# A two-layer decoder trunk on one core: the constants move from 13 loads on GpSimd's queue to 5 on the sync queue, and layer 0's x^T is rounded as it is loaded

## The chip, the cores and the metric

The kernel runs on one core of a Trainium2 chip. The metric is the time of one execution in device microseconds (us). Several executions are timed and the median is given; one more execution is taken with the hardware profiler, and its profile is the one shown here. The engines are named as in the profile: PE (TensorE, matrix products), PEld (its weight loads), DVE (VectorE), ACT (ScalarE), POOL (GpSimd) and SP (SyncE, which only starts transfers). "SPq" and "POOLq" are the queues on which SP and POOL start DMAs.

## What is computed

Two layers of a decoder trunk, on 256 positions of width 2048, in float32. Each layer normalises x, projects it by one large matrix, mixes in four ways side by side, and adds the result, projected back, to x:

```
for l in range(DEPTH):                       # 2
    h = rms_norm(x, norm_g[l])
    p = split_columns(h @ w_in[l])           # 2048 -> 18 column groups, 7700 wide
    fox  = softmax attention with a forget gate,  times silu(fox_g)
    diff = rms_norm(softmax map 1 - lam * softmax map 2) v, times silu(diff_g)
    moba = causal softmax attention with rotary,  times silu(moba_g)
    gla  = rms_norm(chunked gated linear attention), times silu(gla_g)
    x = x + concat(fox, diff, moba, gla) @ w_out[l]      # 2048 -> 2048
return rms_norm(x, final_norm_g)
```

The small parameters beside the two matrices are `fox_fb` (a bias of fox's forget gate), `diff_lam` (from which `lam` is made), `diff_norm_g`, `gla_norm_g`, and `gla_wa2` and `gla_ba` (GLA's gate).

## The kernel before, in words

**Products in float32 by three passes.** PE multiplies rounded numbers (float32r). Each weight tile `raw` is rounded on ACT into `hi` (`hi_of`), and DVE takes the rest, `lo = raw - hi` (`lo_of`). The transposed activations are split in the same way, into the two halves of `hTp`. A product is then hi by hi, lo by hi and hi by lo, 12 matmuls for a step of two k-tiles of 128 and both halves of the rows.

**The plan.** `_steps` (L176) lists the steps in the order in which PE does them. A step is two k-tiles of one block of columns. Layer 0 begins with the three narrow blocks (348, 512 and 348 columns, containing GLA's gate, q, k and fox's forget gate), taken k-tile by k-tile because x^T arrives piece by piece: 24 steps. Then come the blocks named in `MIDDLE` (L40), one after the other, 8 steps each, and the four blocks of `w_out`, whose later k-tiles wait for the later groups in the order gla, fox, diff, moba (`OUT_ORDER`). The first three steps are treated in halves (`HALVED`).

**Pairs and forms.** Some blocks, two in layer 0's and three in layer 1's `NAMES` (L41), are computed two at a time from seven products of sums ("forms", p1 to p7) in place of eight. Their names stand in `MIDDLE` but make no steps of their own. Their steps, 28 for each pair, are put among the others at the places in `FORMS_AT` (L43). The sums of activations that the forms need are made by `sum_forms` (L1687) from the scaled x^T (`env["t", l, c]`) into `mTh` and `mTl`. A second set of weights, `ys`, which lies in the tile `xs`, is loaded by `load_y` (L1549) up to `EARLY` steps ahead of the front of the loads, and changed by DVE and by accumulating DMAs as the forms go on.

**Who orders the other engines.** The program is written out by a planner that keeps a model of time (`Times`, `emit`, `choose`). Between groups of six matmuls, `fill` (L516) gives ACT and DVE work: the rounding of the next steps' weights goes first if it is urgent (`URGENT_HI`, `URGENT_LO`, `split_for`, with `LEAD` for the three-stage splits of p7), and otherwise the heads of the tasks in the order of their ranks (gla, fox, diff, moba). A task's operation is let through once the planner believes its operands ready; for a load that is a modelled landing time (`CONSTANT` is 4.0). The engines then execute their instructions in the order written. `ahead` is 3: a step's weights are rounded at most three steps before PE needs them (`PART_BUFS` is 4).

**The queues.** Weights are loaded by SP (`load`, `load_pair`), six `raw` tiles in a ring, each load waiting for the rounding of what lay in its tile. SP also carries `x^T` (`load_x`), `ys`, and the writes to memory with which tiles are turned (`turned`); POOL's queue carries the reads back, the accumulating loads, and the constants.

**The constants.** The task `constants` (L689) begins once all of layer 0's x^T has been split in the program, at step 16: tables (`ct`: the identity, triangles, rotary tables), fox's bias `fb`, GLA's gate matrix `w3` in float32 (cleared, then six loads), which ACT and DVE round into `wa`. After the first RMS is known come masks, `diff_lam`, `dng`, `neg_b` and `gng`. All 13 loads are on POOL's queue.

**Layer 0's x^T.** It arrives in four chunks `xts[c]` of four k-tiles. For the first four k-tiles, `split_xt` (L1622) rounds with the scale (`norm_g`) in the instruction: `xt_hi` on ACT, `xt_lo` on DVE. For the others, `whole_xt` (L1604) first scales on ACT into a tile `env["t", 0, c]`, which is then rounded whole, two k-tiles at a time. `first_rms` (L1638), which PE's loop moves on once a step, scales the first chunk in the same way, squares each `xts[c]` in place and adds the squares up.

Almost every instruction is recorded at L482, the line in `emit` where operations are written out; the names of the tiles tell them apart. Tiles named `four` are slots of a general pool of 13.

Of the kernel before, what the change touches and what calls it, by code (L numbers as in the profile page):

```python
# [13 lines left out]
F32 = mybir.dt.float32  # L14
# [12 lines left out]
H = 4  # L27
# [9 lines left out]
WARM = (512,) * 7 + (256,)  # L37
HALVED = 3
X_AT = (5, 8, 11, 13)
MIDDLE = (('gla_v', 'diff_q', 'fox_k', 'diff_v', 'fox_q', 'fox_g', 'diff_g', 'diff_k', 'moba_k', 'moba_v', 'moba_q', 'fox_v', 'moba_g'), ('gla_v', 'diff_k', 'fox_k', 'fox_q', 'fox_v', 'moba_q', 'fox_g', 'diff_q', 'diff_g', 'moba_v', 'moba_k', 'moba_g', 'diff_v'))  # L40
NAMES = ((('diff_q', 'diff_k'), ('moba_v', 'diff_v')), (('diff_q', 'diff_k'), ('moba_v', 'diff_v'), ('moba_g', 'diff_g')))  # L41
PAIR = tuple(tuple(3 + MIDDLE[l].index(z) for names in NAMES[l] for z in names) for l in range(2))
FORMS_AT = ((29, 33, 37, 37, 38, 39, 39, 40, 41, 42, 43, 46, 47, 48, 49, 49, 50, 52, 54, 55, 56, 56, 57, 59, 60, 61, 62, 64, 66, 67, 69, 71, 72, 73, 73, 76, 77, 77, 79, 80, 81, 82, 83, 84, 86, 88, 90, 91, 92, 92, 92, 93, 94, 96, 96, 98), (27, 29, 29, 29, 30, 30, 30, 31, 32, 32, 32, 32, 33, 33, 35, 35, 36, 37, 37, 38, 39, 39, 39, 41, 42, 43, 43, 44, 45, 45, 46, 46, 47, 49, 50, 50, 51, 51, 51, 52, 53, 53, 54, 54, 55, 55, 56, 57, 58, 58, 59, 59, 60, 60, 61, 61, 62, 65, 65, 65, 66, 66, 66, 67, 68, 69, 70, 71, 72, 72, 72, 73, 74, 74, 75, 75, 76, 77, 78, 79, 80, 80, 81, 83))  # L43
FORM_ORDER = ("p1", "p5", "p3", "p6", "p7", "p2", "p4")

ADDED_BY_V = ("p1", "p2")
# [13 lines left out]
URGENT_LO = 2.5  # L60
STALL = 0.1
DELAY = 0.5
LEAD = 3.0
OVERLAP = 0.085
SAFE = 1.5
HANDOVER = 0.2
SOON = 0.5
WAITED = 0.3
EARLY = 8
LOADED = 6.0  # L70
WRITE = 7.0
READ = 5.0
# [170 lines left out]
def bcast_rows(ap1d, offset, n):  # L243
    return bass.AP(tensor=ap1d.tensor, offset=ap1d.offset + offset, ap=[[0, P], [1, n]])
# [142 lines left out]
def hybrid_trunk(  # L387
# [3 lines left out]
    xt: bass.AP,  # L391
    norm_gt: bass.AP,
    weights: bass.AP,
    fox_fb: bass.AP,
    diff_lam: bass.AP,
    diff_norm_gt: bass.AP,
    gla_wa2: bass.AP,
    gla_ba: bass.AP,
    gla_norm_gt: bass.AP,
    final_norm_g: bass.AP,  # L400
    const: bass.AP,
    const_b: bass.AP,
# [180 lines left out]
    def matmul(out, lhsT, rhs, start, stop, tiles=1, main=False, **kw):  # L583
        n = int(np.prod(rhs.shape[1:]))
        us = (n * 4 if lhsT.dtype == F32 else n + 32) / 2400.0 / tiles
        give(Op("t", partial(t_.matmul, out, lhsT, rhs, start=start, stop=stop, **kw), [rhs] if main else [lhsT, rhs],
                [] if main else [out], us))
        if main:
            times.end(out, times.now, "t")
# [54 lines left out]
        return z  # L644


    ct = cp.tile([P, CONST["f"].shape[1]], F32, name="ct")
    ngt = cp.tile([P, DEPTH, KT], F32, name="ngt")
    xs = big.tile([P, 2, D], F32, name="xs")

# [8 lines left out]
    fb = cp.tile([P, DEPTH, H], F32, name="fb")  # L659
    dng = cp.tile([P, DEPTH], F32, name="dng")  # L660
    gng = cp.tile([P, DEPTH], F32, name="gng")
# [27 lines left out]
    def constants():  # L689

        yield from until(("h", 0, 3))
        g_.move(ct, const, 4.5)
        g_.move(fb.rearrange("p l h -> p (l h)"), bcast_rows(fox_fb, 0, DEPTH * H), CONSTANT)
        given_out("loaded")
        w3 = s2.get([P, DEPTH, 256])
        g_.memset(w3, 0.0)
        for i in range(0, 96, 32):
            g_.move(w3[i:i + 16], gla_wa2.rearrange("l r e -> r l e"), CONSTANT)
            g_.move(w3[i + 16:i + 17].rearrange("p l e -> p (l e)"), gla_ba.rearrange("(o l) e -> o (l e)", o=1), CONSTANT)
        yield  # L700
        hi_of(wa, w3)
        yield
        lo_of(wa[64:96], w3[64:96], wa[64:96])
        s2.put(w3)
        given_out("constants")
        yield from until(("r", 0))
        c, n = CAT["masks"]
        mb = s4.get([P, n], BF16)
        g_.move(mb, const_b[:, c:c + n], CONSTANT)
        yield  # L710
        v_.tensor_copy(masks.rearrange("p l t -> p (l t)"), mb)
        s4.put(mb)
# [12 lines left out]
        s2.put(lp, lamt)  # L725
        yield
        a_.activation(ls2, ls2, AF.Exp)
        yield
        for l in range(DEPTH):
            li = 0.8 - 0.6 * math.exp(-0.3 * l)  # L730
            v_.scalar_tensor_tensor(lam[:, l:l + 1], ls2[:, l, 0:1], li, ls2[:, l, 1:2], op0=OP.add, op1=OP.subtract)
            v_.tensor_scalar(dng[:, l:l + 1], dng[:, l:l + 1], 1.0 - li, None, op0=OP.mult)
        given_out("lam")

    hTp = big.tile([P, KT, 2, SEQ], F32R, name="hTp")
# [12 lines left out]
    def hi_of(hi, src, scale=1.0):  # L748
        a_.activation(hi, src, AF.Copy, scale=scale)

    def lo_of(lo, src, hi):
        v_.tensor_sub(lo, src, hi.bitcast(F32))
# [884 lines left out]

    def first_rms():  # L1638

        def fold(t):  # L1640
            for n in (2, 1):
                v_.tensor_add(t[:, 0:n], t[:, 0:n], t[:, n:2 * n])

        for c in range(4):
            yield from until(("h", 0, c))
            if WHOLE and c == 0:
                whole_xt(range(4))
            a_.activation(xts[c], xts[c], AF.Square)
            if c in (1, 2):
                v_.tensor_add(xts[0], xts[0], xts[c])  # L1650
                s4.put(xts[c])
            if c > 1:
                fold(xts[0 if c == 2 else 3])
        v_.tensor_add(xts[0][:, 0], xts[0][:, 0], xts[3][:, 0])
        yield
        yield
        yield
        ps = side.get([P, 1024])
        for m in range(2):
            matmul(ps[:, m:m + 1], xts[0][:, 0, m * P:(m + 1) * P], one, True, True)  # L1660
        t = before_pow(ps[:, 0:2], 2, 1.0 / D)
        side.put(ps)
        s4.put(xts[0], xts[3])
        r = sm.tile([P, 2], F32, name="rstd", bufs=2)
        power(r, t, 2)
        know_rows(0, r)
# [20 lines left out]
    def sum_forms(l):  # L1687
# [3 lines left out]
            yield from until(("h", l, c))  # L1691
        yield from until(("r", l))
        yield
        z = yield from s4.take([P, 8, P])
        whole = [env["t", l, c] for c in range(4)] if l or WHOLE else None

        def sums(op, a, b):
            for i in range(2):
# [373 lines left out]
    while tasks:  # L2072
# [3 lines left out]
    final_rows(1, b["ps1"][:, :256])  # L2076


_INS = ["x", "xt", "norm_gt", "weights", "fox_fb", "diff_lam", "diff_norm_gt", "gla_wa2", "gla_ba", "gla_norm_gt",
        "final_norm_g", "const", "const_b"]  # L2080


# [23 lines left out]
```

## Time and profile before

| | us |
|---|---|
| median of 3 timed executions | 891.17 |
| lowest, highest | 890.27, 892.38 |
| the profiled execution | 888.25 |
| its span, first to last instruction | 886.5 |
| busy in it: PE, DVE, ACT, POOL | 871.6, 734.9, 585.3, 65.0 |

How to read the lines below: a row of the timeline or of a single engine gives the start in us from the span's start, the time in us, engine, line and operation, `out<-in`, the shapes, the count of merged instructions, and in brackets how long the engine had been idle and what ended that. A row of a stretch `A:B` gives its length, then the busy time of PE, PEld, DVE, ACT and POOL with the count of instructions, the granted clock of PE (1.00 is full), the mean busy share of the 16 DMA engines, and GB/s. A row of a queue gives packets, MB and the share of the engines' time. A row of waits gives the total in us, how often, and the longest. A row of the DMA issues gives the size of one and the us from issue to landing.

### The profile page before, as it was taken

The page shows a single profiled execution, that of the slowest core. Times are in us where ns is not written, and L with a number is a line of the kernel's source. Part 1 is how long each engine was busy: PE and PEld are TensorE (multiplying, and loading weights), DVE is VectorE, ACT ScalarE, POOL GpSimd, SP SyncE. Part 2 cuts the span into 40 slices and gives each one's busy share as a digit, 9 for nine tenths or more (in the row PEclk, how much of TensorE's full clock was granted, in tenths as well). Part 3 has the DMA queues.
Part 4 walks back from the last instruction along what each step waited for, and adds up shares of the span by engine and source line. Part 5 has one row for each costly group of instructions (what it writes and reads, how often), then busy time and mean ns, then how long its engine had stood idle before and what let it go on. Part 6 is the DMA issues. An engine that isn't in the chain of part 4 may idle for free.

```text
span 886.5 us, 12487 instructions
## 1 busy us (share of the span) xinstructions
PE 871.6 (98%) x4292; PEld 739.1 (83%) x4292; DVE 734.9 (83%) x974; ACT 585.3 (66%) x919; POOL 65.0 (7%) x96
## 2 busy tenths in 40 slices
PE   8999999999999999999999999999999999999896
PEld 5998888888887988888899888888888788888786
DVE  4879979899787997757668699999999998986483
ACT  6877955478586468735756994676667776767361
POOL 3010010001010001000000010001100100100100
PEclk9999999999999999999999999999999999999999
DMA  8878795668997675987879786689898998779822
GB/s 280 304 247 270 233 309 182 205 231 298 377 286 235 201 285 198 313 317 221 279 256 356 240 229 250 209 306 266 247 328 290 278 302 295 247 257 353 281 96 95
DMA packets 84663, 231.63 MB, mean 261 GB/s; under 512 B 9736, under 2 KB 29976, under 8 KB 84472
## 3 DMA queue, kind: packets, MB, share of 16 engines
q1 hardware_dynamic: 75064, 198.29, 65.1%
q0 software_dynamic: 9104, 31.75, 13.5%
q10 hardware_dynamic: 432, 0.80, 0.2%
q8 instruction: 33, 0.54, 0.2%
q14 instruction: 30, 0.25, 0.1%
HBM read 208.25 MB, written 22.55 MB: 260 GB/s over the span
## 4 chain that ended last, share of the span: by engine, by line
PE 93%; DVE 3%; issue 1%; DMA 1%; ACT 0%; SPq 0%; POOLq 0%; POOL 0%; DVEq 0%; ACTq 0%
PE mm L482 79%; PE side L482 14%; DVE lo L482 2%; DMA raw<-in_weights 1%; DVE four L482 1%; DVE tq L482 0%; DVE xs L482 0%; SPq L1596 0%; ACT four L482 0%; DVE eight L482 0%; ACT hi L482 0%; SPq L1543 0%; DVE mTl L482 0%; ACT mTh L482 0%; POOLq L2102 0%
## 5 line engine op out<-in xcount | busy, mean ns | idle before, releaser
L482 ACT ACTIVATE hi<-raw 128x1024 fp32r<-128x1024 f32 (+2 forms) x319 | 316.6, 1009 | 181.2 <-PE mm L482 92.5
L482 DVE TENSOR_TENSOR lo<-raw,hi 128x1024 fp32r<-128x1024 f32 (+2 forms) x319 | 363.0, 1154 | 64.6 <-ACT hi L482 59.1
L482 PE MATMUL mm<-hi,hTp 128*128 128x512 f32 (+1 forms) x1520 | 374.1, 380 | 3.0 <-ACT hi L482 2.6
L482 PEld LDWEIGHTS mm<-hi,hTp 128*128 128x128 f32 x1520 | 277.8, 188 | 55.8 <-ACT hi L482 4.6
L482 PE MATMUL mm<-lo,hTp 128*128 128x512 f32 (+1 forms) x760 | 206.1, 378 | 0.0
L482 PEld LDWEIGHTS mm<-lo,hTp 128*128 128x128 f32 x760 | 139.9, 188 | 25.3 <-DVE lo L482 0.3
L482 PE MATMUL mm<-hi,mTh 128*128 128x512 f32 (+1 forms) x352 | 99.8, 383 | 3.3 <-ACT mTh L482 2.5
L482 PE MATMUL mm<-hi,mTl 128*128 128x512 f32 (+1 forms) x352 | 99.0, 381 | 0.1
L482 PE MATMUL mm<-lo,mTh 128*128 128x512 f32 (+1 forms) x352 | 98.9, 381 | 0.0
L482 ACT ACTIVATE hi<-xs 128x1024 fp32r<-128x1024 f32 x60 | 63.2, 1060 | 20.8 <-PE mm L482 18.3
L482 PEld LDWEIGHTS mm<-hi,mTh 128*128 128x128 f32 x352 | 63.3, 188 | 15.4 <-ACT mTh L482 2.7
L482 PEld LDWEIGHTS mm<-lo,mTh 128*128 128x128 f32 x352 | 64.0, 188 | 13.6 <-DVE lo L482 1.1
L482 PEld LDWEIGHTS mm<-hi,mTl 128*128 128x128 f32 x352 | 64.2, 188 | 13.1 <-DVE mTl L482 0.5
L482 DVE TENSOR_TENSOR lo<-xs,hi 128x1024 fp32r<-128x1024 f32 x60 | 72.0, 1212 | 0.8 <-ACT hi L482 0.7
L482 POOL DMA_DIRECT2D four<-far x40 | 22.1, 553 | 488.6 <-DMA far<-four 174.4
L482 DVE TENSOR_TENSOR xs<-xs,raw 128x1024 f32<-128x1024 f32 x40 | 48.6, 1215 | 0.0
L482 PE MATMUL side<-four,four 128*128 128x128 f32 (+3 forms) x320 | 42.3, 298 | 0.0
L482 PEld LDWEIGHTS side<-four,four 128*128 128x128 f32 (+1 forms) x320 | 38.2, 190 | 4.6 <-issue 1.4
L482 DVE STREAM_TRANSPOSE four<-four 128x1024 f32<-128x1024 f32 (+1 forms) x34 | 38.7, 1140 | 3.7 <-ACT four L482 3.5
L482 ACT ACTIVATE four<-mm,rstd 128x512 f32<-128x512 f32 (+2 forms) x46 | 29.2, 663 | 14.6 <-PE mm L482 14.2
L482 ACT ACTIVATE four<-side 128x128 f32<-128x128 f32 (+3 forms) x66 | 16.0, 266 | 23.8 <-PE side L482 23.2
L482 ACT ACTIVATE four<-side,nb 128x128 f32<-128x128 f32 (+1 forms) x64 | 26.2, 417 | 4.2 <-DVE nb L482 4.2
(152 smaller groups left out, 715.6 us busy)
## 6 DMA issues: line engine op xcount, KB each, us to landing
raw<-in_weights SPq DMA_DIRECT2D x271, 512.0 KB, 5.0
four<-far POOLq DMA_DIRECT2D x34, 512.0 KB, 6.5
far<-four SPq DMA_DIRECT2D x128, 128.0 KB, 3.7
raw<-in_weights SPq DMA_DIRECT2D x46, 348.0 KB, 4.8
xs<-in_weights SPq DMA_DIRECT2D x20, 512.0 KB, 5.5
xs<-in_weights POOLq DMA_DIRECT2D x20, 512.0 KB, 8.7
xs<-in_x SPq DMA_DIRECT2D x4, 512.0 KB, 7.9
kept<-xs SPq DMA_DIRECT2D x1, 2048.0 KB, 8.4
```

The lines of the kernel that those rows point to most:

```text
L482: op.do()
```

## The change

Five things are changed together.

1. **Constants.** `fox_fb` (spread over the partitions), `diff_norm_g` and `gla_norm_g` are appended to the table on the host, so that `ct` is 12 columns wider and one load brings all of them. GLA's gate matrix with its bias is laid out on the host, zeros included, and loaded by one transfer. The loads are `ct`, `w3`, the masks, `diff_lam` and `neg_b`: five, all on SP's queue (`q_`) at the same places in the program.
2. **Layer 0's x^T.** All k-tiles are rounded by `xt_hi` and `xt_lo` straight from `xts`. `first_rms` squares into a tile of its own. A new task `scale_xt` scales each chunk in place after its Square, four instructions a chunk, and `sum_forms` waits for these.
3. **Order of the blocks.** `MIDDLE` is new for both layers.
4. **Places of the forms.** `FORMS_AT` is new: in layer 0 the first places move from 29 to 32 and others by up to three; in layer 1 two places move by one.
5. **Planner.** `LEAD` is 3.5 instead of 3.0, `EARLY` 3 instead of 8.

```diff
-MIDDLE = (('gla_v', 'diff_q', 'fox_k', 'diff_v', 'fox_q', 'fox_g', 'diff_g', 'diff_k', 'moba_k', 'moba_v', 'moba_q', 'fox_v', 'moba_g'), ('gla_v', 'diff_k', 'fox_k', 'fox_q', 'fox_v', 'moba_q', 'fox_g', 'diff_q', 'diff_g', 'moba_v', 'moba_k', 'moba_g', 'diff_v'))
+MIDDLE = (('gla_v', 'fox_k', 'diff_q', 'fox_q', 'diff_v', 'fox_g', 'diff_g', 'moba_v', 'moba_k', 'diff_k', 'fox_v', 'moba_q', 'moba_g'), ('gla_v', 'fox_k', 'diff_k', 'fox_q', 'fox_v', 'moba_q', 'fox_g', 'moba_v', 'diff_q', 'moba_k', 'diff_g', 'moba_g', 'diff_v'))
...
-LEAD = 3.0
+LEAD = 3.5
...
-EARLY = 8
+EARLY = 3
...
     def constants():
 
         yield from until(("h", 0, 3))
-        g_.move(ct, const, 4.5)
-        g_.move(fb.rearrange("p l h -> p (l h)"), bcast_rows(fox_fb, 0, DEPTH * H), CONSTANT)
+        q_.move(ct, const, CONSTANT)
         given_out("loaded")
         w3 = s2.get([P, DEPTH, 256])
-        g_.memset(w3, 0.0)
-        for i in range(0, 96, 32):
-            g_.move(w3[i:i + 16], gla_wa2.rearrange("l r e -> r l e"), CONSTANT)
-            g_.move(w3[i + 16:i + 17].rearrange("p l e -> p (l e)"), gla_ba.rearrange("(o l) e -> o (l e)", o=1), CONSTANT)
+        q_.move(w3.rearrange("p l e -> p (l e)"), gla_w, CONSTANT)
...
-        g_.move(mb, const_b[:, c:c + n], CONSTANT)
+        q_.move(mb, const_b[:, c:c + n], CONSTANT)
...
-        g_.move(lamt.rearrange("p l a d -> p (l a d)"), bcast_rows(diff_lam, 0, DEPTH * 256), CONSTANT)
-        g_.move(dng, diff_norm_gt, CONSTANT)
+        q_.move(lamt.rearrange("p l a d -> p (l a d)"), bcast_rows(diff_lam, 0, DEPTH * 256), CONSTANT)
         c, n = CAT["neg"]
-        g_.move(neg_b, const_b[:, c:c + n], CONSTANT)
-        g_.move(gng, gla_norm_gt, CONSTANT)
+        q_.move(neg_b, const_b[:, c:c + n], CONSTANT)
...
-    def whole_xt(kts):
-
-        for kt in kts:
-            if kt % 4 == 0:
-                env["t", 0, kt // 4] = s4.get([P, 4, SEQ])
-            a_.activation(env["t", 0, kt // 4][:, kt % 4], xts[kt // 4][:, kt % 4], AF.Copy, scale=ngt[:, 0, kt:kt + 1])
+    def scale_xt():
+
+        for c in range(4):
+            yield from until(("squares", c))
+            for k in range(4):
+                kt = c * 4 + k
+                a_.activation(xts[c][:, k], xts[c][:, k], AF.Copy, scale=ngt[:, 0, kt:kt + 1])
+                if k % 2:
+                    yield
+            env["t", 0, c] = xts[c]
+            given_out(("t", c))
...
     def split_xt(kts):
 
-        if WHOLE and kts[0] >= 4:
-            whole_xt(kts)
-            hi, lo = (z[:, kts[0]:kts[-1] + 1] for z in hT)
-            src = env["t", 0, kts[0] // 4][:, kts[0] % 4:kts[-1] % 4 + 1]
-            hi_of(hi, src)
-            lo_of(lo, src, hi)
-        else:
-            for kt in kts:
-                xt_hi(kt)
-            for kt in kts:
-                xt_lo(kt)
+        for kt in kts:
+            xt_hi(kt)
+        for kt in kts:
+            xt_lo(kt)
...
+        sq = {}
         for c in range(4):
             yield from until(("h", 0, c))
-            if WHOLE and c == 0:
-                whole_xt(range(4))
-            a_.activation(xts[c], xts[c], AF.Square)
+            sq[c] = (yield from s4.take([P, 4, SEQ])) if WHOLE else xts[c]
+            a_.activation(sq[c], xts[c], AF.Square)
+            if WHOLE:
+                given_out(("squares", c))
...
     begin(constants(), 0, 3)
+    if WHOLE:
+        begin(scale_xt(), 0, 3)
     begin(sum_forms(0), 0, 3)
```

More of the change, by code (lines that the diff above doesn't have):

```diff
@@ L39 @@
 X_AT = (5, 8, 11, 13)
-MIDDLE = (('gla_v', 'diff_q', 'fox_k', 'diff_v', 'fox_q', 'fox_g', 'diff_g', 'diff_k', 'moba_k', 'moba_v', 'moba_q', 'fox_v', 'moba_g'), ('gla_v', 'diff_k', 'fox_k', 'fox_q', 'fox_v', 'moba_q', 'fox_g', 'diff_q', 'diff_g', 'moba_v', 'moba_k', 'moba_g', 'diff_v'))
+MIDDLE = (('gla_v', 'fox_k', 'diff_q', 'fox_q', 'diff_v', 'fox_g', 'diff_g', 'moba_v', 'moba_k', 'diff_k', 'fox_v', 'moba_q', 'moba_g'), ('gla_v', 'fox_k', 'diff_k', 'fox_q', 'fox_v', 'moba_q', 'fox_g', 'moba_v', 'diff_q', 'moba_k', 'diff_g', 'moba_g', 'diff_v'))
 NAMES = ((('diff_q', 'diff_k'), ('moba_v', 'diff_v')), (('diff_q', 'diff_k'), ('moba_v', 'diff_v'), ('moba_g', 'diff_g')))
 PAIR = tuple(tuple(3 + MIDDLE[l].index(z) for names in NAMES[l] for z in names) for l in range(2))
-FORMS_AT = ((29, 33, 37, 37, 38, 39, 39, 40, 41, 42, 43, 46, 47, 48, 49, 49, 50, 52, 54, 55, 56, 56, 57, 59, 60, 61, 62, 64, 66, 67, 69, 71, 72, 73, 73, 76, 77, 77, 79, 80, 81, 82, 83, 84, 86, 88, 90, 91, 92, 92, 92, 93, 94, 96, 96, 98), (27, 29, 29, 29, 30, 30, 30, 31, 32, 32, 32, 32, 33, 33, 35, 35, 36, 37, 37, 38, 39, 39, 39, 41, 42, 43, 43, 44, 45, 45, 46, 46, 47, 49, 50, 50, 51, 51, 51, 52, 53, 53, 54, 54, 55, 55, 56, 57, 58, 58, 59, 59, 60, 60, 61, 61, 62, 65, 65, 65, 66, 66, 66, 67, 68, 69, 70, 71, 72, 72, 72, 73, 74, 74, 75, 75, 76, 77, 78, 79, 80, 80, 81, 83))
+FORMS_AT = ((32, 33, 35, 38, 39, 40, 41, 42, 43, 44, 45, 46, 47, 48, 49, 50, 52, 53, 54, 55, 56, 57, 58, 59, 60, 61, 62, 64, 67, 68, 69, 71, 72, 73, 73, 76, 77, 77, 79, 80, 81, 82, 83, 84, 86, 88, 90, 92, 93, 93, 93, 93, 95, 96, 97, 99), (27, 29, 29, 29, 30, 30, 30, 31, 32, 32, 32, 32, 33, 33, 35, 35, 36, 37, 37, 38, 39, 39, 39, 41, 42, 43, 44, 44, 45, 45, 46, 46, 47, 49, 50, 50, 51, 51, 51, 52, 53, 53, 54, 54, 55, 55, 56, 57, 58, 58, 59, 59, 60, 60, 61, 61, 62, 65, 65, 65, 66, 66, 66, 67, 68, 69, 70, 71, 72, 72, 72, 73, 74, 74, 75, 75, 76, 78, 78, 79, 80, 80, 81, 83))
 FORM_ORDER = ("p1", "p5", "p3", "p6", "p7", "p2", "p4")
@@ L393, in hybrid_trunk @@
     weights: bass.AP,
-    fox_fb: bass.AP,
     diff_lam: bass.AP,
[L396 to L399, printed above, removed]
+    gla_w: bass.AP,
     final_norm_g: bass.AP,
@@ L644, in put_in_order @@
         return z
-    ct = cp.tile([P, CONST["f"].shape[1]], F32, name="ct")
+    ct = cp.tile([P, CONST["f"].shape[1] + 12], F32, name="ct")
+    own = ct[:, CONST["f"].shape[1]:]
     ngt = cp.tile([P, DEPTH, KT], F32, name="ngt")
@@ L658, in hybrid_trunk @@
     masks = cp.tile([P, NL, 64], U8, name="masks")
-    fb = cp.tile([P, DEPTH, H], F32, name="fb")
+    fb = own[:, :8].rearrange("p (l h) -> p l h", h=H)
     dng = cp.tile([P, DEPTH], F32, name="dng")
-    gng = cp.tile([P, DEPTH], F32, name="gng")
+    gng = own[:, 10:12]
     wa = cp.tile([P, DEPTH, 256], F32R, name="wa")
@@ L731, in constants @@
             v_.scalar_tensor_tensor(lam[:, l:l + 1], ls2[:, l, 0:1], li, ls2[:, l, 1:2], op0=OP.add, op1=OP.subtract)
-            v_.tensor_scalar(dng[:, l:l + 1], dng[:, l:l + 1], 1.0 - li, None, op0=OP.mult)
+            v_.tensor_scalar(dng[:, l:l + 1], own[:, 8 + l:9 + l], 1.0 - li, None, op0=OP.mult)
         given_out("lam")
@@ L1642, in fold @@
                 v_.tensor_add(t[:, 0:n], t[:, 0:n], t[:, n:2 * n])
+        sq = {}
         for c in range(4):
             yield from until(("h", 0, c))
-            if WHOLE and c == 0:
-                whole_xt(range(4))
-            a_.activation(xts[c], xts[c], AF.Square)
+            sq[c] = (yield from s4.take([P, 4, SEQ])) if WHOLE else xts[c]
+            a_.activation(sq[c], xts[c], AF.Square)
+            if WHOLE:
+                given_out(("squares", c))
             if c in (1, 2):
-                v_.tensor_add(xts[0], xts[0], xts[c])
-                s4.put(xts[c])
+                v_.tensor_add(sq[0], sq[0], sq[c])
+                s4.put(sq[c])
             if c > 1:
-                fold(xts[0 if c == 2 else 3])
-        v_.tensor_add(xts[0][:, 0], xts[0][:, 0], xts[3][:, 0])
+                fold(sq[0 if c == 2 else 3])
+        v_.tensor_add(sq[0][:, 0], sq[0][:, 0], sq[3][:, 0])
         yield
@@ L1659, in first_rms @@
         for m in range(2):
-            matmul(ps[:, m:m + 1], xts[0][:, 0, m * P:(m + 1) * P], one, True, True)
+            matmul(ps[:, m:m + 1], sq[0][:, 0, m * P:(m + 1) * P], one, True, True)
         t = before_pow(ps[:, 0:2], 2, 1.0 / D)
         side.put(ps)
-        s4.put(xts[0], xts[3])
+        s4.put(sq[0], sq[3])
         r = sm.tile([P, 2], F32, name="rstd", bufs=2)
@@ L1693, in sum_forms @@
         yield
+        whole = None
+        if l or WHOLE:
+            for c in range(4 if not l else 0):
+                yield from until(("t", c))
+            whole = [env["t", l, c] for c in range(4)]
         z = yield from s4.take([P, 8, P])
-        whole = [env["t", l, c] for c in range(4)] if l or WHOLE else None
         def sums(op, a, b):
@@ L2076, in hybrid_trunk @@
     final_rows(1, b["ps1"][:, :256])
-_INS = ["x", "xt", "norm_gt", "weights", "fox_fb", "diff_lam", "diff_norm_gt", "gla_wa2", "gla_ba", "gla_norm_gt",
-        "final_norm_g", "const", "const_b"]
+_INS = ["x", "xt", "norm_gt", "weights", "diff_lam", "gla_w", "final_norm_g", "const", "const_b"]
 def kernel(**inputs):
@@ L2089 @@
     given["norm_gt"] = np.ascontiguousarray(g.reshape(DEPTH, KT, P).transpose(2, 0, 1))
-    for name in ("diff_norm_g", "gla_norm_g"):
-        given[name + "t"] = np.ascontiguousarray(given.pop(name).T)
+    gla_w = np.zeros((P, DEPTH, 256), np.float32)
+    for i in range(0, 96, 32):
+        gla_w[i:i + 16] = given["gla_wa2"].transpose(1, 0, 2)
+        gla_w[i + 16] = given["gla_ba"]
+    given["gla_w"] = gla_w.reshape(P, -1)
     given["xt"] = np.ascontiguousarray(given["x"][0].T.reshape(KT, P, SEQ).transpose(1, 0, 2))
     given["weights"] = in_steps(given.pop("w_in"), given.pop("w_out"))
-    given["const"], given["const_b"] = CONST["f"], CONST["b"]
+    own = [np.broadcast_to(given["fox_fb"].reshape(1, -1), (P, DEPTH * H)), given["diff_norm_g"].T, given["gla_norm_g"].T]
+    given["const"], given["const_b"] = np.concatenate([CONST["f"], *own], 1), CONST["b"]
     nc = bacc.Bacc("TRN2", target_bir_lowering=False, num_devices=1, dynamic_dma_scratch_size=4096)
```

## The prediction

> **What bounds the kernel now.** I read the page's busy times first, then the busy time by 20 us stretches, then the chain and the timelines of single engines where PE was idle.
>
> ```profile
> PE 871.6 (98%) x4292; PEld 739.1 (83%) x4292; DVE 734.9 (83%) x974; ACT 585.3 (66%) x919; POOL 65.0 (7%) x96
> ```
> ```profile
> 0.00:20.00 20.00, 16.00 (x64) 10.67 (x65) 8.35 (x17) 12.28 (x22) 7.40 (x18) 1.00 0.85 283
> ...
> sum 460.00, PE 456.00 PEld 385.41 DVE 369.18 ACT 308.20 POOL 35.28; mean PE 19.83 PEld 16.76 DVE 16.05 ACT 13.40 POOL 1.53
> ```
> ```profile
> 860.00:886.50 26.50, 19.18 (x160) 18.98 (x159) 10.75 (x24) 4.95 (x9) 2.04 (x3) 0.92 0.21 80
> sum 426.50, PE 415.58 PEld 353.71 DVE 365.70 ACT 277.06 POOL 29.72; mean PE 19.79 PEld 16.84 DVE 17.41 ACT 13.19 POOL 1.42
> ```
>
> PE sets the time. In the first 460 us it is idle for 460.00 - 456.00 = 4.0 us, and all of that lies in the first 20 us (20.00 - 16.00). In the other 426.5 us it is idle for 10.9 us, 7.3 of them in the last 26.5, where the output is written. So work that comes off ACT, DVE or a queue in the middle of the kernel is worth nothing; a stall that goes in the first 20 us is worth its length, because everything behind it is a full PE. The start is the place to look:
>
> ```profile
> 14.46 1.52 PE L482 MATMUL mm<-hi,hTp 128*128 128x348 f32 x8 [0.21 <-ACT hi L482]
> 15.82 0.79 PE L482 MATMUL mm<-lo,hTp 128*128 128x348 f32 x4
> 18.10 2.12 PE L482 MATMUL mm<-hi,hTp 128*128 128x512 f32 x8 [1.49 <-ACT hi L482]
> ```
> ```profile
> 11.54 1.09 ACT L482 ACTIVATE hi<-raw 128x348 fp32r<-128x348 f32 x2 [1.65 <-DMA raw<-in_weights]
> 12.54 0.89 ACT L482 ACTIVATE hTp<-four,ngt 128x256 fp32r<-128x256 f32 x2
> 13.63 0.79 ACT L482 ACTIVATE hi<-raw 128x696 fp32r<-128x696 f32 x1 [0.19 <-DMA raw<-in_weights]
> 14.32 1.69 ACT L482 ACTIVATE four<-four,ngt 128x256 f32<-128x256 f32 x4
> 16.04 1.06 ACT L482 ACTIVATE four<-four 128x1024 f32<-128x1024 f32 x1
> 17.01 1.72 ACT L482 ACTIVATE hi<-raw 128x1024 fp32r<-128x1024 f32 x2
> 18.63 0.89 ACT L482 ACTIVATE four<-four,ngt 128x256 f32<-128x256 f32 x2
> 19.55 0.63 ACT L482 ACTIVATE hTp<-four 128x512 fp32r<-128x512 f32 x1
> ```
>
> These are steps 3 and 4 of the plan. Up to 13.6 us each rounding on ACT waits for its weights to land (1.65 us, 0.19 us): the DMA sets the pace. Then ACT does four scalings of x^T and a Square (14.32 to 17.10) ahead of the rounding that step 4 needs, and PE, done with step 3 at 15.82 + 0.79 = 16.61, stands for 1.49 us.
>
> **The change part by part.**
>
> *The four scalings leave the start.* They took ACT from 14.32 to 16.04, 1.72 us. The Square stays, now into a tile of its own. The rounding for step 4 then starts at 17.01 - 1.72 = 15.29 instead of 17.01. PE took it up 18.10 - 17.01 = 1.09 us after it began, so it could begin at 16.38; it is busy with step 3 until 16.61. What is late next is PE itself, so the gain is the whole gap and no more: **1.49 us**.
>
> *Eight loads of the constants leave the start.* Before, they stand in GpSimd's queue, which has nothing to wait for, and so run at once, although the program puts them behind step 16.
>
> ```profile
> ct<-in_const POOLq DMA_DIRECT2D x1, 289.0 KB, 6.3
> ```
> ```profile
> q0 software_dynamic: 132, 0.32, 33.4%
> ```
> ```profile
> DMA packets 803, 1.83 MB, mean 366 GB/s; under 512 B 201, under 2 KB 280, under 8 KB 803
> ...
> q1 hardware_dynamic: 631, 1.74, 97.7%
> q0 software_dynamic: 172, 0.09, 7.0%
> ```
>
> The first of the two answers is of 5 to 10 us, the second of 10 to 15 us. q0 is GpSimd's queue, q1 SP's. q0's packets take 33.4% of 5 us and 7.0% of 5 us of all sixteen engines, 1.67 + 0.35 = 2.02 us, just while the weights of steps 1 to 3 are awaited. By bytes it is less: 0.41 MB at 366 GB/s is 1.12 us. I price the relief from 0 (see the rivals) to 2.02 us and take the middle of the two prices from the trace, **1.57 us**; the engine time counts the small packets as the engines felt them, the bytes are the price if others fill their gaps. It adds to the 1.49: landings that come earlier by some amount move step 3 (its rounding starts when its weights land), step 3's end and with it step 4 by the same amount. Sum at the start: 1.49 + 1.57 = 3.06 us, between 1.49 and 3.51.
>
> The Trainium skill ("DMA: Bandwidth & Descriptors", Issuing engines are not separate DMA queues) says that transfers started by any engine run on the same 16 DMA engines and interleave, so that several queues save only issue time. The 33.4% agrees that they share, and by that rule alone the other queue is worth nothing, and the sum would be 1.49 us; what I count is that the SP queue carries these loads later, not that it carries them better.
>
> *The same loads on SP's queue.* SP reaches them among the weights of the steps after 16. Five issues on an engine that mostly waits cost nothing:
>
> ```profile
> SPq L482 <- DVE lo L482: 371.2, 194, 8.2
> ```
> ```profile
> 48.42 1.06 ACT L482 ACTIVATE hi<-raw 128x1024 fp32r<-128x1024 f32 x1 [0.82 <-PE side L482]
> 50.30 0.79 ACT L482 ACTIVATE hi<-raw 128x696 fp32r<-128x696 f32 x1 [0.82 <-PE mm L482]
> 50.99 0.61 ACT L482 ACTIVATE wa<-four 128x512 fp32r<-128x512 f32 x1
> ```
>
> But a load behind weights in a queue in order can come late, and ACT (rounding wa) and DVE (casting the masks) wait for it in order, with the roundings of weights queued behind them and PE behind those. ACT is held by PE here (0.82 us before each rounding): it has filled its part buffers and runs about three steps of 1.88 us (50.30 - 48.42) ahead, 5.6 us of cover. At worst SP stands for its longest wait, 8.2 us, and the load takes the 6.3 us of ct: 14.5 - 5.6 = 8.9 us of stall; at best 0. There is no gain here, since nothing waited for these loads before. I take 0, because the planner lets a task's rounding through only when its load should have landed, and keep the rest as a rival.
>
> *Rounding x^T as it is loaded.* For each pair of k-tiles ACT had 0.89 us of scaling and 0.63 us of rounding (18.63, 19.55); the rounding with the scale in it is 0.89 us (12.54), so 0.63 us goes, six times, 3.8 us. On DVE:
>
> ```profile
> 13.10 0.88 DVE L482 SCALAR_TENSOR_TENSOR hTp<-four,ngt,hTp 128x256 fp32r<-128x256 f32 x2
> ...
> 20.22 0.69 DVE L482 TENSOR_TENSOR hTp<-four,hTp 128x512 fp32r<-128x512 f32 x1
> ```
>
> 0.88 for 0.69, six times, 1.1 us more. The sixteen scalings (about 7 us) come back later as fillers. All of it lies beside a PE that is full from 18.10 on. Without that cover the 1.1 us of DVE would be the loss. The scaled tiles feed the forms, which have room:
>
> ```profile
> 83.62 1.22 DVE L482 TENSOR_TENSOR mTl<-four,mTh 128x1024 fp32r<-128x1024 f32 x1
> ```
> ```profile
> 106.91 0.61 PE L482 MATMUL mm<-hi,mTh 128*128 128x512 f32 x2
> ```
>
> The last form is there at 84.84, its kind is first used at 106.91: 22 us of room.
>
> *The places.* Of the new order of layer 1 nothing is left once the paired names, which make no steps of their own, are taken out: it is the same list. In layer 0 one thing remains: fox_v and moba_q change places. PE's work is the same either way. fox_v comes earlier and is no risk. moba_q comes a block later, and the mixing by w_out needs moba's result:
>
> ```profile
> 285.15 1.50 ACT L482 ACTIVATE four<-mm,rstd 128x512 f32<-128x512 f32 x2
> ...
> 310.51 0.97 ACT L482 ACTIVATE four<-mm,rstd 128x348 f32<-128x348 f32 x2
> ```
> ```profile
> 398.89 1.23 DVE L482 TENSOR_TENSOR mTl<-four,mTh 128x1024 fp32r<-128x1024 f32 x1
> ```
> ```profile
> 405.85 1.07 PE L482 MATMUL mm<-hi,mTh 128*128 128x512 f32 x4
> ```
> ```profile
> 775.32 0.69 ACT L482 ACTIVATE four<-mm,rstd 128x512 f32<-128x512 f32 x1 [0.75 <-PE mm L482]
> ```
> ```profile
> 839.18 1.19 PE L482 MATMUL mm<-hi,mTh 128*128 128x512 f32 x4 [2.47 <-ACT mTh L482]
> ```
>
> moba_q is read out at 285.15 and moba's share is ready at 398.89 + 1.23 = 400.12, a way of 115.0 us, 5.7 us ahead of its use at 405.85. In the place of fox_v it is read out at 310.51, so 405.85 - 310.51 = 95.3 us are left. That the way can be shorter shows layer 1, where moba_k is the last: read out at 775.32, and at 839.18 PE, which waited for it, takes its share up, 63.9 us. The need is nearer to the 115.0 than to the 63.9, but 63.9 is the same work with little queued ahead of it, and fox leaves the engines earlier here; I take a stall of 0, with 115.0 - 95.3 = 19.7 us as the end of it. The places of the forms move by up to three steps, LEAD by 0.5 us, and EARLY holds the loads of the forms' y back by five steps; none of them changes what PE does, and with PE never idle between 20 and 460 us they gain nothing. A wait that they brought, or took away, I bound by the one large wait that PE has after the start, the 2.47 us at 839.18. From 2.5 us less to 2.5 us more, then; I take 0, since the order of layer 1's blocks is unchanged and with it what moba waits for.
>
> **Sum.** -1.49 - 1.57 = -3.06 us. The profiled execution took 888.25 us (span 886.5); it would take 885.2. The median of the runs shown is 891.17, 2.9 us above it; a saving at the start has nothing to do with that distance, so I take it off the median: 891.17 - 3.06 = **888.1 us**, 0.34% less. A measurement of this kernel can tell about 0.2%, 1.8 us, from no change.
>
> **The rivals.**
>
> *The freed DMA time goes to others.* What lands late at the start may be held by how long one transfer is on its way and not by the engines' share. For it speaks that the engines had room just then:
>
> ```profile
> 6.00:8.00 2.00, 1.93 (x9) 1.20 (x9) 1.31 (x3) 0.63 (x1) 2.00 (x5) 1.00 0.80 197
> ```
>
> A share of 0.80 and 197 GB/s while weights were awaited. Against it, from 10 to 15 us q1 alone takes 97.7% of them. Then only the scalings count: 891.17 - 1.49 = 889.7 us, within 0.2%. This is also what comes out by the rule of the Trainium skill above. Chance 0.18.
>
> *moba comes late (slower).* If moba's way in layer 0 shrinks by less than 19.7 us, PE stands ahead of the last quarter of w_out. It decides from a way of 95.3 us; the saving is gone at 98.4, and beyond 100.2 the kernel is slower by over 0.2%. For a way half between 95.3 and 115.0, 105.2 us, the time is 888.1 + 9.9 = 898.0 us. For it: moba is the last in the order of ranks, and took 115.0 us with the same engines. Against it: the 63.9 us of layer 1. Chance 0.10.
>
> *The constants hold ACT or DVE near 45 to 60 us.* From a lateness of 5.6 us PE feels it, up to 8.9 us: 888.1 to 897.0, at its middle 892.6. Against it: the cover of 5.6 us is nearly what ct took to land beside full engines, 6.3 us, and the planner holds the task back besides. Chance 0.12, half of it within 0.2%, half slower.
>
> *More than that:* the stall of 2.47 us in layer 1 goes as well, 888.1 - 2.5 = 885.6 us. Nothing in the change aims at it. Chance 0.08.
>
> **How the numbers follow.** The forecast has 0.52, and its own range is 887.7 (relief 2.02) to 889.1 (relief 0.5), about 1 us wider for the scatter of medians (the three runs lie from 890.27 to 892.38). Faster by over 0.2%: 0.52 + 0.08 = 0.60. Within: 0.18 + 0.06 = 0.24. Slower: 0.10 + 0.06 = 0.16. The range goes from 885.5, which holds the case with the stall gone, to 892.5, which holds the freed DMA case and half of the late constants; moba's case and the rest of the constants' stay out, under 0.2.
>
> **What would show it.** Right: on ACT no scaling between the roundings of steps 3 and 4, PE's gap ahead of step 4 gone, no packets of q0 before 15 us, step 3's weights landed at 11.6 to 12.5 instead of 13.6, step 4 on PE at about 15 instead of 18.10, and from there each row of PE about 3 us earlier, up to the end. Wrong: step 3's rounding still at 13.6 (the relief was none); ACT or DVE idle up to DMA w3 or the masks, with PE idle after it, at 40 to 60 us; PE waiting for mTh near 400 us; or a scaling that the planner puts back ahead of the rounding of step 4.

## The result, and the profile after

The kernel after takes 886.18 us in the median of six runs (885.13 to 887.78), the kernel before beside it 890.72 (889.51 to 892.38). The ratio is 0.9949, with a 95% interval of 0.9934 to 0.9963: 4.5 us less, between 3.3 and 5.9. Timed once more, beside 889.19, it took 884.70, ratio 0.9948 [0.9935, 0.9961]. The executions that were profiled took 887.78 us (the longest of its six) and 888.25 (shorter than all six of before), so I compare rows and not spans.

First the page's busy line, and two stretches (columns: stretch, length, busy us of PE, weight load, DVE, ACT and POOL with their instructions, granted clock, DMA share, GB/s).

```profile
PE 871.4 (98%) x4292; PEld 740.2 (84%) x4292; DVE 735.6 (83%) x980; ACT 585.4 (66%) x925; POOL 57.6 (6%) x82
```
```profile
0.00:20.00 20.00, 18.49 (x87) 14.20 (x88) 11.50 (x24) 14.90 (x27) 2.65 (x9) 1.00 0.88 308
0.00:460.00 460.00, 458.49 (x2228) 389.11 (x2229) 371.15 (x504) 312.13 (x501) 27.93 (x43) 1.00 0.80 265
```

PE has the same work. In the first 460 us it is now idle for 460.00 - 458.49 = 1.5 us, where it was 4.0, again all of it in the first 20 us. The start, on ACT and then on PE:

```profile
9.21 0.97 ACT L478 ACTIVATE hi<-raw 128x348 fp32r<-128x348 f32 x2 [1.37 <-DMA raw<-in_weights]
10.08 0.89 ACT L478 ACTIVATE hTp<-four,ngt 128x256 fp32r<-128x256 f32 x2
10.88 0.77 ACT L478 ACTIVATE hi<-raw 128x696 fp32r<-128x696 f32 x1
11.55 1.04 ACT L478 ACTIVATE four<-four 128x1024 f32<-128x1024 f32 x1
12.63 0.51 ACT L478 ACTIVATE four<-four,ngt 128x256 f32<-128x256 f32 x1
13.04 1.04 ACT L478 ACTIVATE hi<-raw 128x1024 fp32r<-128x1024 f32 x1
```
```profile
12.38 1.44 PE L478 MATMUL mm<-hi,hTp 128*128 128x348 f32 x8
13.66 0.80 PE L478 MATMUL mm<-lo,hTp 128*128 128x348 f32 x4
14.29 2.01 PE L478 MATMUL mm<-hi,hTp 128*128 128x512 f32 x8
```

Step 3's rounding begins at 10.88 instead of 13.63, 2.75 us earlier, and no longer waits for its weights. One of the four scalings (12.63) still stands ahead of step 4's rounding (13.04). PE goes from step 3 to step 4 without a gap and begins it at 14.29 instead of 18.10: 3.81 us earlier. Step 3 itself begins only 14.46 - 12.38 = 2.08 us earlier on PE, although its rounding gained 2.75: it no longer waits for the rounding, and what is late there is now PE. The DMA queues from 5 to 10 us, and SP's issues, after and then before:

```profile
q1 hardware_dynamic: 824, 1.49, 92.0%
```
```profile
4.98 1.56 SPq L478 DMA_DIRECT2D raw<-in_weights  x3
6.59 0.68 SPq L1534 DMA_DIRECT2D four<-in_xt  x1
```
```profile
5.00 2.93 SPq L482 DMA_DIRECT2D raw<-in_weights  x3
7.97 0.83 SPq L1543 DMA_DIRECT2D four<-in_xt  x1
```

GpSimd's queue (q0, 33.4% before) is gone from the answer, and SP's own packets take 92.0% of the engines. The last two fences show what I had not priced: SP issues the same three loads in 1.56 us, which took 2.93 before.

How far does the shift reach? In this execution PE is 4.14 us early at 621 us (the first row is of before, the second of after). Then 1.9 us are lost at one place (ACT, then PE), and 0.59 at 832.31, where PE waits for a read-back from DRAM too. The last row is PE's wait in the tail:

```profile
625.62 0.70 PE L482 MATMUL mm<-hi,mTh 128*128 128x512 f32 x2 [0.74 <-DVE four L482]
```
```profile
621.48 0.70 PE L478 MATMUL mm<-hi,mTh 128*128 128x512 f32 x2 [0.74 <-DVE four L478]
```
```profile
652.98 1.06 ACT L478 ACTIVATE four<-four 128x1024 f32<-128x1024 f32 x1 [4.78 <-DMA four<-far]
```
```profile
654.53 1.21 PE L478 MATMUL mm<-hi,hTp 128*128 128x512 f32 x4 [1.50 <-ACT four L478]
...
837.50 2.07 PE L478 MATMUL mm<-hi,mTh 128*128 128x512 f32 x4 [2.47 <-ACT mTh L478]
```

ACT stands in order before a tile that comes back from DRAM, with the roundings of weights behind it. The tail's 2.47 us of waiting for mTh, which the prediction priced at 839.18, is the same to the digit and comes 1.68 us earlier. A second profile of the same kernel (below) loses nothing at 654 us.

### The profile page after: what moved, and what is told of

It is laid out like the page before. It is cut to its first block, busy times and chain, and to the rows that moved or that the text cites. A ratio compares the mean times of both kernels' runs of the same rounds, so it can differ in the third digit from the quotient of the medians.

```text
span 886.0 us, 12490 instructions
## 1 busy us (share of the span) xinstructions
PE 871.4 (98%) x4292; PEld 740.2 (84%) x4292; DVE 735.6 (83%) x980; ACT 585.4 (66%) x925; POOL 57.6 (6%) x82
## 4 chain that ended last, share of the span: by engine, by line
PE 90%; DVE 5%; DMA 2%; issue 1%; ACT 1%; SPq 0%; POOLq 0%; POOL 0%; DVEq 0%
PE mm L478 77%; PE side L478 13%; DVE lo L478 2%; DVE four L478 1%; DMA four<-far 1%; DVE raw L478 1%; DMA far<-four 0%; DMA raw<-in_weights 0%; ACT hi L478 0%; ACT four L478 0%; DVE tq L478 0%; DVE xs L478 0%; DVE eight L478 0%; SPq L478 0%; DVE side L478 0%
```

## The experiments

Runs that stand together below were timed beside the same runs of the kernel before. Theory A: the start sets the gain, by the scalings that go and by the constants' bytes that no longer move beside the first weights. Its rivals are named with each run.

**One part at a time.** Three runs make one part of the change each, on the kernel before: the constants (part 1), x^T (part 2), the places and leads (parts 3 to 5). A fourth is the kernel after with its five loads issued by GpSimd's queue. Of each a few lines:

```diff
-        g_.move(ct, const, 4.5)
+        q_.move(ct, const, CONSTANT)
...
```
```diff
-    def whole_xt(kts):
+    def scale_xt():
...
+    if WHOLE:
+        begin(scale_xt(), 0, 3)
```
```diff
-LEAD = 3.0
+LEAD = 3.5
...
-EARLY = 8
+EARLY = 3
```
```diff
-        q_.move(ct, const, CONSTANT)
+        g_.move(ct, const, CONSTANT)
...
```

> Only the constants are changed (five loads on the sync queue); x^T, the order of blocks, the places of the forms, LEAD and EARLY are those of before. Theory A (the loads on GpSimd's queue took DMA time while the weights of steps 1 to 3 were awaited, and their going moves those weights): step 3's rounding starts at about 11 us instead of 13.6, the four scalings and the Square still stand ahead of step 4's rounding, so PE begins step 4 at about 15.4 instead of 18.10 with a gap of about 1 us left ahead of it; the kernel is about 2.7 us faster than before. Theory B (the freed DMA time goes to other transfers): step 3's rounding stays at 13.6 and the time within 0.5 us of before.

> Only the handling of layer 0's x^T is changed; the 13 loads stay on GpSimd's queue and the places are those of before. Theory A: step 3's rounding stays at 13.6 us, PE begins step 4 at 16.6 instead of 18.10, and the kernel is 1.5 us faster, no more. Theory C (the whole gain is ACT's, whose queue is shorter everywhere in the first 50 us): 3 us or more faster, with the later steps gaining on top of step 4.

> Only the order of blocks, the places of the forms, LEAD and EARLY are changed. Theory A (PE is full in the middle whatever the order): the start is unchanged to 0.1 us and the time within 1 us of before. Theory D (the places bring what the measured 4.5 us has above the 3.9 us by which PE is early after step 5): 0.6 us or more faster. The rival of the prediction (moba late): PE waits for mTh near 405 us, slower by the wait.

> The changed kernel with its five loads on GpSimd's queue instead of the sync queue. GpSimd has nothing to wait for, so the table and the gate matrix (0.55 MB, more bytes than the eight loads of before) move in the first 15 us again. Theory A (what counts is when the bytes move): step 3's rounding starts at 13 us or later, and of the 4.5 us at most 1.5 to 2 us are left. Theory E (what counts is that there are few large loads, or none of the cleared tile's small ones): step 3's rounding starts at about 11 to 12 us and the time is within 1 us of the changed kernel.

Beside 889.50 us: constants alone 897.09, ratio 1.0086 [1.0065, 1.0107]; x^T alone 888.78, 0.9990 [0.9981, 1.0000]; places alone 889.97, 1.0001 [0.9989, 1.0012]; five loads on GpSimd's queue 888.96, 0.9994 [0.9980, 1.0008].

x^T behaves nearly as theory A said, which had step 4 at 16.6 and 1.5 us. PE in that run:

```profile
16.82 1.45 PE L482 MATMUL mm<-hi,hTp 128*128 128x512 f32 x5 [0.26 <-ACT hi L482]
```

Step 4 begins 1.28 us earlier, and theory C, 3 us or more, falls. With the places alone step 3's rounding came at 13.88 and step 4 at 18.35, 0.25 us later than before, with no PE wait near 405 us; so two profiles can differ by a quarter of a microsecond at the start, and theory D falls. With the five loads on GpSimd's queue step 3's rounding came at 12.86, near the 13 of theory A and not the 11 to 12 of theory E. The constants alone were a miss: they make the kernel 7.6 us slower, and none of the theories had that. Yet their start gained what theory A said: PE's step 4 began at 15.19, and theory B falls. So some 10 us were lost later, and I had to find out why.

**Is it the loads, or the order that the planner writes?** `emit` keeps a modelled landing time for every load, and `choose` picks ACT's and DVE's next instruction by it. Whoever moves a load thus rewrites the program far beyond it. In the run with the constants alone both things changed at once, and in the one with GpSimd's queue too. The next four keep them apart: the planner is told one thing, and the load is issued on another queue, so that PE, ACT and DVE run the very list of instructions of another kernel (in the four traces the lists are the same but for the names of a few tiles).

```diff
-        q_.move(ct, const, CONSTANT)
+        c_move(ct, const, CONSTANT)
...
+    def c_move(out, src, us, n=None):
+        op = Op("dq", partial(nc.gpsimd.dma_start, out, src), [src], [out], us)
+        op.moved = (n or int(np.prod(out.shape))) * 4 / RATE
+        give(op)
```

For the old order the planner is told of the thirteen loads of before, and SP issues five:

```diff
-        g_.move(ct, const, 4.5)
-        g_.move(fb.rearrange("p l h -> p (l h)"), bcast_rows(fox_fb, 0, DEPTH * H), CONSTANT)
+        c_move(ct, const, 4.5, P * CONST["f"].shape[1])
+        no_move("fb", P * 8, CONSTANT)
...
```

Here `c_move` gives the planner a load of GpSimd's and issues it on SP's queue, and `no_move` gives it a load that is not issued at all. The held-back run adds, ahead of the first load on GpSimd's queue:

```diff
+        give(Op("do", lambda: nc.gpsimd.tensor_copy(held, hTp[:, 15, 1, 0:1].bitcast(F32))))
```

> The five loads on the sync queue, everything else as before, and (unlike the earlier run with the constants alone) with every instruction of PE, ACT, DVE in the order of before: the planner is told the old thirteen loads, so it lays out the same program. Theory O (the 7 us that the constants alone lost came from the other order that the planner then laid out, not from the loads): the start's gain is kept, 886.0 to 888.2 us, 1.5 to 3.5 below before. Theory L (constants that land at 40 to 50 us make DVE or ACT late between 60 and 300 us): slower than before, 892 to 897 us, with waits of PE for DVE in that stretch.

> The kernel after with its five loads issued by GpSimd's queue, every instruction of PE, ACT and DVE in the order of after. Theory A (what counts is that the constants' bytes no longer move beside the first weights): step 3's rounding about 2 us later than in after, PE's step 4 near 16.1 us, and the end later by 1.8 to 3.5 us, 888 to 889.7 us. Rival P (the new order of the work is what gained): as after, within 0.7 us, 885.5 to 887 us.

> The run with the constants alone (897.1 us), in its very order of PE, ACT and DVE, but with the five loads issued by GpSimd's queue, so that they land before 15 us. Theory O (that order is slow whatever queue loads the constants): as slow or slower by the start's 2 to 3 us, 896 to 901 us. Theory L (it was the late landing): the loss goes, 887 to 890 us.

> The kernel after in its own order with the five loads on GpSimd's queue, behind one GpSimd copy of a column of layer 0's last rounded x^T chunk, so that they start near 40 us as in after. Theory A (when the bytes move): as after, 885.3 to 887.2 us, the first 20 us as in after. Rival Q (which queue issues them): as with the five loads on GpSimd's queue at the start, 888 to 890 us.

Beside 889.92 us: the five loads on SP's queue in the old order 888.02, ratio 0.9977 [0.9966, 0.9987]; on GpSimd's queue in the new order 888.10, 0.9976 [0.9966, 0.9986]; on GpSimd's queue in the order of the run with the constants alone 898.05, 1.0097 [1.0081, 1.0113]; held back on GpSimd's queue 885.94, 0.9964 [0.9950, 0.9978].

Theory O holds and theory L falls. The kernel with the same five loads on the same queue is 2 us faster than before in the old order and was 7.6 us slower in the order that the planner wrote for them; and that order costs as much when the loads land early. The two runs with the loads on GpSimd's queue in the new order have one order and one queue and differ only in when the loads start (and in one small copy on GpSimd): 888.10 against 885.94, and at the last wait of the tail 837.64 against 835.18. The intervals of their ratios overlap a little, but the held-back run lies where theory A put it and outside the 888 to 890 us of rival Q, which falls: what counts is when the bytes move, not whose queue moves them. The start of the run in the old order, SP, ACT and PE:

```profile
4.97 1.38 SPq L478 DMA_DIRECT2D raw<-in_weights  x3
6.40 0.67 SPq L1554 DMA_DIRECT2D four<-in_xt  x1
```
```profile
10.57 0.77 ACT L478 ACTIVATE hi<-raw 128x696 fp32r<-128x696 f32 x1
11.24 1.70 ACT L478 ACTIVATE four<-four,ngt 128x256 f32<-128x256 f32 x4
12.97 1.06 ACT L478 ACTIVATE four<-four 128x1024 f32<-128x1024 f32 x1
```
```profile
15.03 2.11 PE L478 MATMUL mm<-hi,hTp 128*128 128x512 f32 x8 [1.02 <-ACT hi L478]
```

By the constants alone step 3's rounding comes 13.63 - 10.57 = 3.06 us earlier and step 4 18.10 - 15.03 = 3.07. The four scalings (1.70) are still there, and so is a gap of 1.02 us: that part belongs to x^T. The 3.07 us last: the wait in the tail ends at 836.17, 3.01 us earlier than before, while the medians show 1.9. The run with five loads at the start on GpSimd's queue, DMA from 5 to 10 us, SP, and ACT:

```profile
q1 hardware_dynamic: 591, 0.96, 57.7%
q0 software_dynamic: 156, 0.56, 38.1%
```
```profile
4.97 1.74 SPq L478 DMA_DIRECT2D raw<-in_weights  x3
```
```profile
13.12 0.77 ACT L478 ACTIVATE hi<-raw 128x696 fp32r<-128x696 f32 x1
```

And ACT in the run with those loads held back:

```profile
11.57 0.77 ACT L478 ACTIVATE hi<-raw 128x696 fp32r<-128x696 f32 x1
```

Five loads instead of thirteen, at the old time, give step 3 only 13.63 - 13.12 = 0.51 us; starting them later gives another 1.55. Against theory A's "first 20 us as in after" this start is 0.69 us late (11.57 against 10.88), and PE's step 4 begins at 14.83 with a wait of 0.29 us, though nothing of GpSimd's queue moves before 41 us. Why is open; the seven profiles with the loads on SP's queue have 10.42 to 10.88.

**Do the new places matter, and do the parts add?** The kernel after with the four old lines of places and leads; the old order with SP's five loads and, besides, the new x^T; the kernel after with the old x^T; and the kernel after again, unchanged. A few lines of each of the three edits, the first and third on the kernel after, the second on the run in the old order:

```diff
-LEAD = 3.5
+LEAD = 3.0
...
-EARLY = 3
+EARLY = 8
```
```diff
-    def whole_xt(kts):
+    def scale_xt():
...
```
```diff
-    def scale_xt():
+    def whole_xt(kts):
...
```

> The kernel after with the four lines of places and leads (MIDDLE, FORMS_AT, LEAD, EARLY) as before; constants and x^T as after. PE's order is then, instruction for instruction, that of the run with the constants alone (897.1 us). Theory O (that order is what costs, and the new places are what takes it away): that run less x^T's 0.7 to 1.5 us, 894.5 to 897.5 us, with PE's waits for DVE near 140 to 227 us again. Rival N (places matter as little here as they did by themselves): 885.5 to 887.5 us.

> The five loads on the sync queue and x^T as after, with PE's instructions in the order of before (the planner is told the old thirteen loads; ACT and DVE differ from before by x^T's instructions alone). Theory S (the two parts add, and the new places only keep a good order): 2.06 and 0.9 us below before, 886.3 to 888 us, no gap of PE in the first 20 us. Rival G (the new order gives some of the time itself): 887.5 to 889 us, a microsecond or more above after in this batch.

> The kernel after with x^T as before (scaled into a copy, four scalings ahead of step 4's rounding); PE's order differs from after's by two rows. Theory S: x^T's part is missing, 0.7 to 1.5 us above after in this batch, PE's step 4 near 15.1 us with about 1 us of waiting. Rival X (beside the constants' relief x^T gives nothing, since DMA no longer holds step 4): within 0.5 us of after.

> The kernel after once more, on the chip of the other three. Theory R (the 1.50 us that PE waited at 654 us in its first profile was one late landing of a read-back, not the order): that wait is under 0.6 us, and the shift of about 4 us goes on past 700 us; 885.3 to 887 us. Rival H (the order holds it there): 1.2 to 1.8 us of waiting at that place again.

Beside 889.19 us: old places 894.08, ratio 1.0054 [1.0040, 1.0068]; both parts in the old order 885.98, 0.9961 [0.9946, 0.9977]; old x^T 886.95, 0.9971 [0.9959, 0.9983]; after again 884.70, 0.9948 [0.9935, 0.9961].

With the old places the changed kernel would be 9.4 us slower than it is, and slower than before (the time is 0.4 us under what I expected); at the last wait of the tail it is 843.52 - 835.43 = 8.1 us later. PE in that run, and in the run with the same order and the loads on GpSimd's queue:

```profile
143.02 0.70 PE L478 MATMUL mm<-hi,mTh 128*128 128x512 f32 x2 [0.86 <-DVE four L478]
...
159.05 0.73 PE L478 MATMUL mm<-lo,mTh 128*128 128x512 f32 x2 [1.24 <-DVE lo L478]
...
167.22 0.73 PE L478 MATMUL mm<-lo,mTh 128*128 128x512 f32 x2 [1.07 <-DVE lo L478]
...
223.57 1.21 PE L478 MATMUL mm<-hi,hTp 128*128 128x512 f32 x4 [1.53 <-DVE four L478]
```
```profile
162.28 0.74 PE L478 MATMUL mm<-lo,mTh 128*128 128x512 f32 x2 [1.24 <-DVE lo L478]
...
170.46 0.73 PE L478 MATMUL mm<-lo,mTh 128*128 128x512 f32 x2 [1.04 <-DVE lo L478]
```

The same instructions wait for the same time, wherever the loads are issued. I look for the root earlier, on DVE. Its timeline in the run with the old places, and then two stretches of that run and of the run with both parts in the old order (after the length come PE, PEld and, third, DVE):

```profile
114.13 0.75 DVE L478 SCALAR_TENSOR_TENSOR four<-mm,rstd,four 128x512 f32<-128x512 f32 x1 [3.57 <-PE mm L478]
```
```profile
80.00:100.00 20.00, 20.00 (x92) 16.64 (x91) 17.89 (x22) 15.38 (x23) 0.70 (x1) 1.00 0.84 276
100.00:120.00 20.00, 20.00 (x90) 16.57 (x89) 15.87 (x30) 16.04 (x19) 4.06 (x5) 1.00 1.01 258
```
```profile
80.00:100.00 20.00, 20.00 (x91) 16.61 (x91) 19.72 (x36) 18.54 (x27) 0.00 (x0) 1.00 0.72 235
100.00:120.00 20.00, 20.00 (x90) 16.57 (x89) 19.76 (x37) 13.05 (x16) 4.08 (x5) 1.00 1.00 254
```

In this order the planner has put an instruction that needs a result of PE where DVE then stands for 3.57 us in order. From 80 to 120 us DVE does 33.76 us of work in place of 39.48; PE is still full. By 140 us DVE has made up 2.7 of the 5.7 us (17.59 us of work from 120 to 140 us against 14.86). From then on PE waits for what DVE should have made, residues of weights and tiles of the mixing: 0.86 + 1.24 + 1.07 + 1.53 = 4.70 us. The whole loss against the old order is 894.08 - 885.98 = 8.1 us in the medians and 843.52 - 835.00 = 8.5 us at the last wait of the tail. Beside the 4.70 us, 0.32 are lost at the start and 0.62 in two shorter waits; the other 2.9 lie in rows that count as busy, and I did not place them. That the wait at 114 us causes the later ones is argued from the rows and not shown: two shorter waits of DVE (0.79 us at 91.44, 1.27 at 95.07) come ahead of it, PE's own order differs too, and in the kernel before DVE stands even longer, 4.86 us at 130.09, and PE loses nothing.

The second profile of the kernel after, ACT and PE:

```profile
651.12 1.06 ACT L478 ACTIVATE four<-four 128x1024 f32<-128x1024 f32 x1 [3.16 <-DMA four<-far]
```
```profile
659.00 1.17 PE L478 MATMUL mm<-hi,hTp 128*128 128x512 f32 x4 [0.23 <-DVE four L478]
...
835.43 1.21 PE L478 MATMUL mm<-hi,mTh 128*128 128x512 f32 x4 [2.47 <-ACT mTh L478]
```

The read-back came earlier and PE did not wait: theory R. The shift is 4.14 us at 659 us (663.14 before) and 3.75 in the tail. Both parts in the old order reach that last wait at 835.00, so by the traces theory S holds: the two parts make the gain, and the new places only keep an order as good as the old one. The medians differ by 1.28 us (885.98 and 884.70), the microsecond that rival G asked for, but the intervals of their ratios overlap. In the two profiles that difference lies behind the last wait, where both run the same 264 matmuls: PE is busy with them for 41.25 us at a mean granted clock of 0.92 in the one and for 39.95 us at 0.96 in the other. So these profiles give the new order no gain of its own. The old x^T costs 2.25 us beside the other parts by the medians, more than the 0.7 to 1.5 expected. By the rows it costs 0.96 us at step 4 (15.02 against 14.06) and 0.78 at the last wait (836.21 against 835.43), and the tails differ by the clock again. Rival X, within 0.5 us, falls either way.

The kernel after stayed the fastest; no experiment beat it.

## Why the prediction was right

The forecast was 3.06 us less, and it was 4.5 (3.3 to 5.9), inside the range and with the right sign; the rows of the second profile account for 3.75. The start was the right place and both terms were real. That the number fell inside the range is in part luck: 886.18 us lies below the forecast's own range, 887.7 to 889.1, and also below that with its 1 us of scatter. The whole range reached down to 885.5 only for the rival in which the 2.47 us stall of layer 1 goes, and that stall stayed. Point by point:

- *The bound.* Right. In the second profile PE idles outside the start as before, but for 0.34 us at 830 us, and what the start gained was still there as 4.14 us at 659 us and 3.75 in the tail. In the first profile a late read-back took 1.9 us of it.
- *The four scalings, 1.49 us.* Nearly right. Alone, x^T's part moved step 4 by 1.28 us, because one scaling stayed ahead of the rounding, as the last lines of the prediction feared; the whole kernel won 0.7 us, or 0.9 by the ratio's mean (0 to 1.7). Beside the other parts it won 2.25 us by the medians, and 0.96 at step 4 by the rows; 1.49 lies between.
- *The constants' relief, 1.57 us between prices of 1.12 and 2.02.* This is the term that was mis-sized. On ACT the rounding of step 3 gained 3.06 us with the old order and 2.75 in the changed kernel, above the upper price. The first step that failed is the sentence that takes the engines' time of q0's packets as the end. What the further 0.7 to 1.0 us is stays open. Beside those packets SP's issue was slower as well, 2.93 us for three loads against 1.38, and x^T's chunk was issued at 7.97 instead of 6.40; but in the three profiles with thirteen loads the rounding does not follow the issue (2.93, 2.31 and 2.37 us of issue, rounding at 13.63, 13.55 and 13.88), so this is a candidate and not shown. The second is the sentence that the landings move step 3, its end and step 4 by the same amount: in the changed kernel step 3 gains 2.08 us on PE and its last row 2.16 (13.66 against 15.82), since PE is then the late one. With 1.65 us at the gap ahead of step 4 that makes the 3.81.
- *The rival of the freed DMA time* fell; 889.7 was its time. What is worth some 2 us is the time at which the loads run (2.2 by the medians, 2.46 at the last wait, 1.1 by the ratios); held back on GpSimd's queue they cost about as little as on SP's (ratio 0.9964 against 0.9949, the intervals overlap). The Trainium skill ("DMA: Bandwidth & Descriptors", Issuing engines are not separate DMA queues) says that transfers share the same 16 engines whichever engine started them. The runs agree, since they show no worth of the queue as such; that this rule alone would give 889.7 was my reading of it.
- *The constants on SP's queue hold ACT or DVE.* Did not happen; wa's rounding ran at 47.08 without a wait.
- *moba late in layer 0.* Did not happen; the first use of its share came at 401.65 (405.85 before), without a wait. moba_q was read out at 307.69, so that a way of 94.0 us was enough. The 2.47 us of layer 1 stayed in every profile.
- *The places, 0.* The number was right (places alone 1.0001) and its reason too narrow. I compared the lists of steps and found them alike, and did not see that moving the loads changes the planner's clock, that this alone rewrites the orders of PE and DVE, and that with the old places 8 us and more are then lost. That the new places kept a good order is luck as far as the prediction goes. A rival with that price belonged on the list: constants moved, places left, 894 to 897 us.

## What to carry to other kernels

At a start that waits for DMA, look at which queue has nothing to wait for: its loads ran first here, wherever the program puts them, and holding back what is needed later was worth 3.0 us at the last wait, more than the 2.02 us of engine time of its packets. Where a planner with a model of time writes the order, a moved load is not a local edit: time the change with the order kept, by telling the planner the old times, and then with the order free. When the engine that is the bound waits for an operand, follow it back to where its maker stood, here some 30 us earlier, and try that place by itself, which I did not do.

## What the runs showed that I had not expected

The issue of a load on SP took longer while GpSimd's queue had loads under way: three loads took 2.31 to 2.93 us in the three profiles with thirteen loads there, 1.74 to 1.91 in the three with five, and 1.38 to 1.66 in the eight with none. The landing of a read-back from DRAM at one place of one program differed by 1.9 us between two executions (652.98 and 651.12), and only the later one cost PE time. The last 264 matmuls, from the wait of 2.47 us on, are the same in all 14 profiles. They kept PE busy for 39.93 to 39.95 us in three of them, whose mean granted clock was 0.998 (before, the loads on SP's queue in the old order, after again), and for 41.02 to 41.53 us in the other eleven, at 0.994 to 0.996. No part of the change touches them, and so neither a profile's span nor the median of a few runs tells much about one microsecond.
